# Separate waits for ScalarE's copy of B's rows and for VectorE's turns in a LoRA kernel

## The chip, the cores and the metric

The kernel runs on one core of a Trainium2 chip. The metric is device time in microseconds (us) of one execution; a lower time is better. A core has five engines that run programs of their own and meet only at semaphores: TensorE (PE in the profile, its weight loads PEld), VectorE (DVE), ScalarE (ACT), GpSimd (POOL) and SyncE (SP), which here issues all transfers between the chip's memory (HBM) and the on-chip buffer SBUF.

## What is computed

```
x: 16 x 512 x 768, A: 768 x 16, B: 16 x 768, scale = 0.5     (float32)
lora = np.matmul(np.matmul(x, A), B)
return (x + scale * lora).astype(np.float32)
```

x is 25.17 MB and is read once; the output is as large and is written once. The arithmetic between is small.

## The kernel before, in words

The 8192 rows (tokens) of x are cut into 64 tiles of 128 tokens; 8 tiles make a group, and there are NG = 8 groups. SBUF has room for 48 tiles, so x comes in by 8 loads (load 0 and load 1 hold group 0; loads 2, 3 and 4 a group each; load 5 two groups; loads 6 and 7 groups 6 and 7) and leaves by 5 stores (0 and 1 a group each, 2, 3 and 4 two groups each). The result is written in place over x, and loads 6 and 7 go into the room that stores 0 and 1 have emptied.

For each group g the work goes through five steps, each on an engine of its own:

1. The casts (`narrowed`, line 196): ScalarE casts tiles 0 to 3 of the group to fp16, GpSimd tiles 4 to 7. Each waits for its load and for `s_taken` >= g, which says that group g-1's fp16 copy `xn` has been turned and that PE has begun to read the turned tile `xt`. For ScalarE line 194 leaves this wait out at g = 1. Each cast raises `s_narrow`.
2. The turn (`turned`, line 256): VectorE transposes `xn` to `xt` in one instruction, and raises `s_turned`.
3. The projection (`projected`, line 286): 24 matmuls of `xt` with `w_bd`, a block-diagonal form of A, into the PSUM tile `ps_yt`. The second raises `s_taken`, the last `s_y`.
4. The muls (line 241): ScalarE writes the scaled projection to `y_bd` in four instructions. The first also raises `s_narrow` (not in the last group), the last `s_spread`.
5. The raising matmuls (`raised`, line 307) multiply `y_bd` with `b_mm` into two PSUM tiles `lora`, two token tiles at a time (a pair), and VectorE's four adds per group (line 261) add them to x in place. The last add of the groups at which a store ends raises `s_sum`.

VectorE's order is written out by hand (lines 271 to 276): the turn of group g+1 stands ahead of the four adds of group g. Its turn waits for `s_narrow` >= 3(g+1): two casts and the first mul of group g, which stands for the end of group g's projection, since `xt` may be overwritten only then. ScalarE's order is: cast of group g+1, muls of group g. PE's loop (lines 328 to 335) runs per group: pairs 0 and 1, the first half of the next projection, pairs 2 and 3, the second half.

B's rows come in at the start, GpSimd casts them (line 214), and PE spreads them over the partitions with two matmuls on `pick` (line 320) into `lora`'s first tile. ScalarE copies them out to `b_mm` (line 234). Before the change this copy waits for `s_taken` >= 1, which the second projection matmul of group 0 raises; PE runs in order, so the matmuls at line 320 are over by then. `b_mm` is waited for once, at line 327, ahead of PE's loop.

SyncE's program (lines 136 to 184) holds all transfers in one order: loads 0 to 5 at the start; stores 0 and 1 when `s_sum` has counted two and PE has raised pair 1 of group 2 (`s_lora` >= 10); load 6 when store 0 has landed, load 7 when store 1 has; store 2 when `s_sum` has counted three and `s_raise` six (PE has begun to raise group 5); store 3 when `s_sum` has counted four; the last store (line 356) after the last add.

Of the kernel before, what the change touches and what calls it, by code (L numbers as in the profile page):

```python
# [28 lines left out]
def kernel(  # L29
# [8 lines left out]
    nc = tc.nc  # L38
# [10 lines left out]
    NG = sum(PARTS) // GROUP  # L49
# [33 lines left out]
    def sem(name):  # L83
        sems.append(nc.alloc_semaphore(name))
        return sems[-1]
# [10 lines left out]
    def memory(t2, i, s, n):  # L96
        S = PARTS[i]
        return t2[ds(parts[i], S * P), :].rearrange("(p s) d -> p s d", s=S)[:, ds(s, n), :]

    def held(i, s, n):  # L100
        return tiles(where.index((i, s)), n)

    def tiles(t, n):
        return x_all[:, ds(t % ROOM, n), :]
# [6 lines left out]
    def load_of(t):  # L111
        i, s = where[t]
        return next(k for k, ld in enumerate(LOADS) if ld[0] == i and ld[1] <= s < ld[1] + ld[2])
# [1 line left out]
    assert SETS * SET == NC  # L115
    s_a, s_b = sem("s_a"), sem("s_b")
    s_ready, s_brows, s_pick = sem("s_ready"), sem("s_brows"), sem("s_pick")
    s_w, s_bh, s_bm = sem("s_w"), sem("s_bh"), sem("s_bm")
    s_first, s_narrow, s_turned, s_taken = sem("s_first"), sem("s_narrow"), sem("s_turned"), sem("s_taken")
    s_y, s_spread, s_lora = sem("s_y"), sem("s_spread"), sem("s_lora")  # L120

# [66 lines left out]
    def narrowed(e, copy, g, first, n=SUB):  # L188
        t = g * GROUP + first
        for k in dict.fromkeys(load_of(t + k) for k in range(n)):  # L190
            if (e, k) not in here:
                here.add((e, k))
                e.wait_ge(s_load[k], 16)
        if g > (e is nc.scalar):
            e.wait_ge(s_taken, g)
        ins = copy(out=xn[:, ds(first, n), :], in_=tiles(t, n))  # L196

        ins.then_inc(s_narrow if g else s_first if first else s_a, 1)

    def on_gpsimd(e):  # L200
        e.memset(a_rows[0:Q], 0.0).then_inc(s_ready, 1)  # L201
        e.memset(b_rows, 0.0).then_inc(s_brows, 1)  # L202
        e.memset(pick, 0.0).then_inc(s_pick, 1)
        e.memset(w_bd.rearrange("p c k m -> p (c k m)").bitcast(fp32), 0.0)  # L204
        e.memset(y_bd.rearrange("p s m -> p (s m)").bitcast(fp32), 0.0).then_inc(s_ready, 1)  # L205
        e.wait_ge(s_pick, 1)
        e.affine_select(  # L207
            out=pick, in_=pick, compare_op=mybir.AluOpType.not_equal, fill=1.0, base=0,
            pattern=[[0, NQ], [-APART, Q]], channel_multiplier=1,
        ).then_inc(s_pick, 1)  # L210
        narrowed(e, e.tensor_copy, 0, 0, SUB // 2)
        e.wait_ge(s_pick, 2)
        e.wait_ge(s_b, 16)
        e.tensor_copy(out=b_half, in_=b_rows).then_inc(s_bh, 1)  # L214
        e.wait_ge(s_ready, 3)
        e.tensor_copy(  # L216
            out=w_one.rearrange("i (c e) k r -> i c e (k r)", c=SETS),
            in_=a_t[0:Q].rearrange("i k r (e c) -> i c e (k r)", c=SET)[:, 0:SETS, 0:SET, :],
        ).then_inc(s_w, 1)
        e.wait_ge(s_w, 1)  # L220
        for b in range(NQ):
            e.tensor_copy(  # L222
                out=w_bd[ds(b * Q, Q), :, :, ds(b * Q, R)], in_=w_one
            ).then_inc(s_w, 1)
            e.wait_ge(s_w, b + 2)
        for g in range(1, NG):
            narrowed(e, e.tensor_copy, g, SUB)

    def on_scalar(e):
        narrowed(e, e.copy, 0, SUB // 2, SUB // 2)  # L230
        narrowed(e, e.copy, 0, SUB)

        e.wait_ge(s_taken, 1)
        e.copy(out=b_mm, in_=lora[0][:, 0, :]).then_inc(s_bm, 1)  # L234
        for g in range(NG):
            if g + 1 < NG:
                narrowed(e, e.copy, g + 1, 0)
            e.wait_ge(s_y, g + 1)
            for b in range(NQ):
                q = ds(b * Q, Q)  # L240
                last = e.mul(out=y_bd[q, :, q], in_=y_ps[q, :, :], mul=sc)  # L241
                if b == 0 and g + 1 < NG:

                    last.then_inc(s_narrow, 1)
            last.then_inc(s_spread, 1)

    def on_vector(e):
        e.wait_ge(s_a, SETS * 16 + 1)
        e.transpose(  # L249
            out=a_t[0:Q].rearrange("i k r c -> i (k r) c"),  # L250
            in_=a_rows[0:Q].rearrange("c (i k r) -> c (k r) i", k=2, r=R),
        ).then_inc(s_ready, 1)

        def turned(first, n):
            ts = [v[:, ds(first, n), :].bitcast(fp32) for v in (xt, xn)]
            return e.transpose(out=ts[0], in_=ts[1])  # L256

        def summed(g, p):
            xs = tiles(g * GROUP + 2 * p, 2)
            e.wait_ge(s_lora, g * PAIRS + p + 1)  # L260
            ins = e.tensor_tensor(out=xs, in0=xs, in1=lora[p % 2], op=mybir.AluOpType.add)  # L261
            if p + 1 == PAIRS and g in STORED:
                ins.then_inc(s_sum, 1)
            elif g + 1 < NG or p + 2 < PAIRS:
                ins.then_inc(s_free[p], 1)

        for h in range(2):
            e.wait_ge(s_first, h + 1)
            ins = turned(h * SUB, SUB)
        ins.then_inc(s_turned, 1)  # L270
        for g in range(NG):
            if g + 1 < NG:
                e.wait_ge(s_narrow, 3 * (g + 1))
                turned(0, GROUP).then_inc(s_turned, 1)
            for p in range(PAIRS):
                summed(g, p)

    def on_tensor(e):


        xv = xt.rearrange("p s (c j k) -> p s c j k", c=NC, k=2)

        def projected(first, last):
            for m in range(first, last):
                c, k = divmod(m, 2)
                mm = e.matmul(  # L286
                    y_ps, w_bd[:, c, k, :], xv[:, :, c, :, k],
                    start=(m == 0), stop=(m == MMS - 1),
                )
                if m == 0:  # L290
                    mm.then_inc(s_turned, -1)
                if m == 1:

                    mm.then_inc(s_taken, 1)
                if m == MMS - 1:
                    mm.then_inc(s_y, 1)

        def raised(p):
            if p == 0:
                e.wait_ge(s_spread, 1)  # L300
            free = s_free[(p + 2) % PAIRS]
            e.wait_ge(free, 1)
            t = lora[p % 2]
            mms = []
            for k in range(2):
                for n0, w in ((0, 512), (512, 256)) if k == 0 else ((0, 256), (256, 512)):
                    mms.append(e.matmul(  # L307
                        t[:, k, ds(n0, w)], y_bd[:, 2 * p + k, :], b_mm[:, ds(n0, w)],
                        start=True, stop=True,
                    ))  # L310
            if p == 0:
                mms[0].then_inc(s_raise, 1)
                mms[2].then_inc(s_spread, -1)
            mms[1].then_inc(free, -1)
            mms[-1].then_inc(s_lora, 1)

        e.wait_ge(s_pick, 2)
        e.wait_ge(s_bh, 1)
        for n0, w in ((0, 512), (512, 256)):
            last = e.matmul(  # L320
                lora[0][:, 0, ds(n0, w)], pick.rearrange("p b r -> p (b r)"),
                b_half[:, ds(n0, w)], start=True, stop=True,
            )
        e.wait_ge(s_w, 1 + NQ)
        e.wait_ge(s_turned, 1)
        projected(0, MMS)
        e.wait_ge(s_bm, 1)
        with e.Fori(0, NG - 1):
            raised(0)
            raised(1)  # L330
            e.wait_ge(s_turned, 1)
            projected(0, MMS // 2)
            raised(2)
            raised(3)
            projected(MMS // 2, MMS)
        for p in range(PAIRS):
            raised(p)

    on_sync(nc.sync)
    on_gpsimd(nc.gpsimd)  # L340
    on_scalar(nc.scalar)
    on_vector(nc.vector)
    on_tensor(nc.tensor)

    nums = [s.num for s in sems]
# [10 lines left out]
    last = nc.sync.dma_start(out=memory(out2, *STORES[-1]), in_=held(*STORES[-1]))  # L356
# [39 lines left out]
```

## Time and profile before

| | us |
|---|---|
| median of 3 runs (123.65 to 123.83) | 123.83 |
| the profiled execution | 123.56 |
| its span, first to last instruction | 121.6 |
| VectorE busy | 81.9 |
| PE busy | 51.1 |
| ScalarE busy | 37.4 |
| GpSimd busy | 28.4 |

The profile is one execution. Its times are given from the span's start; what lies around the span is 123.56 - 121.6 = 1.96 us. A row of the timeline has start, duration, engine, line, operation, tile written <- tiles read, and in brackets how long the engine was idle before and what ended it ("<-"). A row "x4" stands for four instructions in a row, its duration from the first's start to the last's end. In the view by stretches the columns are named in its first line, with the busy time of each engine in us; the DMA share is that of the 16 DMA engines, booked where a packet starts, so that it can pass 1. "DMA to landing" is the time from the start of an issue to the moment at which all its data is there. A small q behind an engine's name (ACTq) marks its sequencer, which runs standing waits (EVENT_SEMAPHORE) itself.

### The profile page before, as it was taken

The page shows a single profiled execution, that of the slowest core. Times are in us where ns is not written, and L with a number is a line of the kernel's source. Part 1 is how long each engine was busy: PE and PEld are TensorE (multiplying, and loading weights), DVE is VectorE, ACT ScalarE, POOL GpSimd, SP SyncE. Part 2 cuts the span into 40 slices and gives each one's busy share as a digit, 9 for nine tenths or more (in the row PEclk, how much of TensorE's full clock was granted, in tenths as well). Part 3 has the DMA queues.
Part 4 walks back from the last instruction along what each step waited for, and adds up shares of the span by engine and source line. Part 5 has one row for each costly group of instructions (what it writes and reads, how often), then busy time and mean ns, then how long its engine had stood idle before and what let it go on. Part 6 is the DMA issues. An engine that isn't in the chain of part 4 may idle for free.

```text
span 121.6 us, 888 instructions
## 1 busy us (share of the span) xinstructions
PE 51.1 (42%) x322; PEld 29.9 (25%) x322; DVE 81.9 (67%) x42; ACT 37.4 (31%) x43; POOL 28.4 (23%) x24
## 2 busy tenths in 40 slices
PE   0000239477457457747745725894574520000000
PEld 0000026244233324424423412552342110000000
DVE  0002950799999999999999969999996992000000
ACT  4003919535417402826240093634004000000000
POOL 7731638135017002606200080620000000000000
PEclk9999999999999999999999998599999998555555
DMA  3999999999998997999999999998999899899890
GB/s 59 436 430 449 445 420 428 445 420 420 477 517 356 420 517 315 428 428 445 420 420 445 436 412 485 420 517 372 404 517 404 372 517 404 372 517 420 356 517 0
DMA packets 1928, 50.43 MB, mean 415 GB/s; under 512 B 236, under 2 KB 236, under 8 KB 392
## 3 DMA queue, kind: packets, MB, share of 16 engines
q1 hardware_dynamic: 1928, 50.43, 97.0%
HBM read 25.26 MB, written 25.17 MB: 415 GB/s over the span
## 4 chain that ended last, share of the span: by engine, by line
DVE 32%; DMA 29%; PE 12%; ACT 9%; issue 1%; SPq 0%; POOLq 0%
DMA x_sb<-in_x_dram 20%; DVE x_sb L261 19%; DVE xt L256 12%; DMA out_dram<-x_sb 9%; PE ps_yt L286 8%; ACT xn L196 6%; PE lora_ps L307 4%; ACT y_bd L241 3%; SPq L139 0%; SPq L391 0%; POOLq L134 0%; POOLq L377 0%
## 5 line engine op out<-in xcount | busy, mean ns | idle before, releaser
L261 DVE TENSOR_TENSOR x_sb<-x_sb,lora_ps 128x1536 f32<-128x1536 f32 x32 | 53.8, 1736 | 1.5 <-PE lora_ps L307 1.4
L307 PE MATMUL lora_ps<-b_mm,y_bd 128*128 128x512 f16 (+1 forms) x128 | 25.1, 329 | 22.2 <-ACT y_bd L241 14.8
L196 ACT CAST xn<-x_sb 128x3072 f16<-128x3072 f32 (+1 forms) x9 | 23.4, 2609 | 34.5 <-DMA x_sb<-in_x_dram 21.7
L286 PE MATMUL ps_yt<-xt,w_bd 128*128 128x256 f16 x192 | 26.5, 291 | 12.9 <-DVE xt L256 12.9
L256 DVE STREAM_TRANSPOSE xt<-xn 128x3072 f32<-128x3072 f32 (+1 forms) x9 | 27.1, 3007 | 6.6 <-ACT y_bd L241 6.1
L196 POOL CAST xn<-x_sb 128x3072 f16<-128x3072 f32 (+1 forms) x8 | 20.7, 2586 | 45.1 <-DMA x_sb<-in_x_dram 23.4
L286 PEld LDWEIGHTS ps_yt<-xt,w_bd 128*128 128x128 f16 x192 | 19.1, 102 | 21.1 <-issue 16.2
L307 PEld LDWEIGHTS lora_ps<-b_mm,y_bd 128*128 128x128 f16 x128 | 10.6, 97 | 34.8 <-ACT y_bd L241 17.0
L241 ACT ACTIVATE y_bd<-ps_yt 32x256 f16<-32x256 f32 x32 | 12.0, 374 | 18.1 <-PE ps_yt L286 17.7
L249 DVE STREAM_TRANSPOSE a_t<-a_rows 32x1024 f32<-32x1024 f32 x1 | 2.0, 1975 | 11.3 <-DMA a_rows<-in_A_dram 11.3
L320 PE MATMUL lora_ps<-b_half,pick 128*128 128x512 f16 (+1 forms) x2 | 0.8, 501 | 12.5 <-POOL b_half L214 12.5
L320 PEld LDWEIGHTS lora_ps<-b_half,pick 128*128 128x128 f16 x2 | 0.1, 105 | 12.5 <-issue 12.5
L222 POOL COPY w_bd<-w_one 32x384 f16<-32x384 f16 x4 | 2.0, 500 | 0.2
L214 POOL CAST b_half<-b_rows 128x768 f16<-128x768 f32 x1 | 0.8, 827 | 4.4 <-DMA b_rows<-in_B_dram 4.4
L234 ACT CAST b_mm<-lora_ps 128x768 f16<-128x768 f32 x1 | 0.8, 799 | 2.6 <-PE ps_yt L286 2.6
L196 ACT ACT_TABLE_LOAD x1 | 1.3, 1283 | 0.9 <-PEq L377 0.9
L204 POOL MEMSET w_bd<- 128x1536 f32 x1 | 1.4, 1372 | 0.0
L201 POOL MEMSET a_rows<- 32x1024 f32 x1 | 0.9, 941 | 0.5 <-POOLq L134 0.5
L216 POOL CAST w_one<-a_t 32x384 f16<-32x384 f32 x1 | 0.9, 851 | 0.9 <-DVE a_t L249 0.9
L202 POOL MEMSET b_rows<- 128x768 f32 x1 | 0.7, 727 | 0.0
L205 POOL MEMSET y_bd<- 128x512 f32 x1 | 0.5, 514 | 0.0
L207 POOL TENSOR_SCALAR_AFFINE_SELECT pick<-pick 128x128 f16<-128x128 f16 x1 | 0.3, 298 | 0.0
(5 smaller groups left out, 0.6 us busy)
## 6 DMA issues: line engine op xcount, KB each, us to landing
out_dram<-x_sb SPq DMA_DIRECT2D x3, 6144.0 KB, 19.0
x_sb<-in_x_dram SPq DMA_DIRECT2D x5, 3072.0 KB, 14.6
x_sb<-in_x_dram SPq DMA_DIRECT2D x1, 6144.0 KB, 41.7
out_dram<-x_sb SPq DMA_DIRECT2D x2, 3072.0 KB, 14.4
x_sb<-in_x_dram SPq DMA_DIRECT2D x1, 2304.0 KB, 9.9
x_sb<-in_x_dram SPq DMA_DIRECT2D x1, 768.0 KB, 4.7
a_rows<-in_A_dram SPq DMA_DIRECT2D x3, 16.0 KB
b_rows<-in_B_dram SPq DMA_DIRECT2D x1, 48.0 KB, 7.5
```

The source lines that it names most:

```text
L196: ins = copy(out=xn[:, ds(first, n), :], in_=tiles(t, n))
L201: e.memset(a_rows[0:Q], 0.0).then_inc(s_ready, 1)
L204: e.memset(w_bd.rearrange("p c k m -> p (c k m)").bitcast(fp32), 0.0)
L216: e.tensor_copy(out=w_one.rearrange("i (c e) k r -> i c e (k r)", c=SETS), in_=a_t[0:Q].rearrange("i k r (e c) -> i c e (k r)", c=SET)[:, ...
L222: e.tensor_copy(out=w_bd[ds(b * Q, Q), :, :, ds(b * Q, R)], in_=w_one).then_inc(s_w, 1)
L241: last = e.mul(out=y_bd[q, :, q], in_=y_ps[q, :, :], mul=sc)
L249: e.transpose(out=a_t[0:Q].rearrange("i k r c -> i (k r) c"), in_=a_rows[0:Q].rearrange("c (i k r) -> c (k r) i", k=2, r=R),).then_inc(s_r ...
L256: return e.transpose(out=ts[0], in_=ts[1])
L261: ins = e.tensor_tensor(out=xs, in0=xs, in1=lora[p % 2], op=mybir.AluOpType.add)
L286: mm = e.matmul(y_ps, w_bd[:, c, k, :], xv[:, :, c, :, k], start=(m == 0), stop=(m == MMS - 1),)
L307: mms.append(e.matmul(t[:, k, ds(n0, w)], y_bd[:, 2 * p + k, :], b_mm[:, ds(n0, w)], start=True, stop=True,))
L320: last = e.matmul(lora[0][:, 0, ds(n0, w)], pick.rearrange("p b r -> p (b r)"), b_half[:, ds(n0, w)], start=True, stop=True,)
```

## The change

ScalarE's copy of B's rows gets a semaphore of its own, `s_bp`, raised by the last matmul at line 320. ScalarE's cast of group 1 now waits for `s_taken` >= 1 like GpSimd's (line 194), as the copy no longer does so ahead of it. The first mul no longer raises `s_narrow`; VectorE's turn waits for `s_y` >= g+1 and for `s_narrow` >= 2(g+1). An instruction carries one wait; a second wait becomes an instruction of its own ahead of it, so ScalarE's program has one instruction more and VectorE's seven. The order of all other instructions on every engine is the same.

```diff
-    s_w, s_bh, s_bm = sem("s_w"), sem("s_bh"), sem("s_bm")
+    s_w, s_bh, s_bp, s_bm = sem("s_w"), sem("s_bh"), sem("s_bp"), sem("s_bm")
...
-        if g > (e is nc.scalar):
+        if g:
             e.wait_ge(s_taken, g)
         ins = copy(out=xn[:, ds(first, n), :], in_=tiles(t, n))
...
         narrowed(e, e.copy, 0, SUB)
-
-        e.wait_ge(s_taken, 1)
+        e.wait_ge(s_bp, 1)
         e.copy(out=b_mm, in_=lora[0][:, 0, :]).then_inc(s_bm, 1)
...
                 last = e.mul(out=y_bd[q, :, q], in_=y_ps[q, :, :], mul=sc)
-                if b == 0 and g + 1 < NG:
-
-                    last.then_inc(s_narrow, 1)
             last.then_inc(s_spread, 1)
...
             if g + 1 < NG:
-                e.wait_ge(s_narrow, 3 * (g + 1))
+                e.wait_ge(s_y, g + 1)
+                e.wait_ge(s_narrow, 2 * (g + 1))
                 turned(0, GROUP).then_inc(s_turned, 1)
...
                 b_half[:, ds(n0, w)], start=True, stop=True,
             )
+        last.then_inc(s_bp, 1)
         e.wait_ge(s_w, 1 + NQ)
```

## The prediction

> **What bounds the kernel now.** I read the page first: the span, the DMA rows, the chain.
>
> ```profile
> span 121.6 us, 888 instructions
> ...
> DMA  3999999999998997999999999998999899899890
> ...
> q1 hardware_dynamic: 1928, 50.43, 97.0%
> ...
> DVE 32%; DMA 29%; PE 12%; ACT 9%; issue 1%; SPq 0%; POOLq 0%
> ```
>
> Two answers stand against each other here. The last line, the chain of waits, gives VectorE 32% and DMA 29%, as if the adds and turns set the end. The lines above it say that the DMA engines are busy in 97.0% of the span and move 50.43 MB, and that none of 40 slices but the first and the last is under 0.7. To choose between them I ask whether the transfers ever wait for the computation. The timeline of SyncE, which issues all transfers, gives the issue times; the views of single issuing lines give the time from an issue to its landing.
>
> ```profile
> 0.89 0.85 SPq L139 DMA_DIRECT2D x_sb<-in_x_dram  x2
> ...
> 44.15 0.82 SPq L149 DMA_DIRECT2D out_dram<-x_sb  x2
> 55.12 7.70 SPq L139 DMA_DIRECT2D x_sb<-in_x_dram  x2
> 74.55 9.02 SPq L149 DMA_DIRECT2D out_dram<-x_sb  x2
> 101.84 0.33 SPq L356 DMA_DIRECT2D out_dram<-x_sb  x1
> ```
>
> ```profile
> DMA to landing us min/median/max: 14.6/14.6/14.6
> ```
>
> ```profile
> DMA to landing us min/median/max: 17.0/17.0/17.0
> ```
>
> ```profile
> DMA to landing us min/median/max: 23.1/23.1/23.1
> ```
>
> ```profile
> DMA to landing us min/median/max: 19.0/19.0/19.0
> ```
>
> These are, in order, the views of load 7, store 2, store 3 and the last store (line 356), each alone. A row of two issues gives the second by its end: load 7 is issued 0.3 us before 55.12 + 7.70 = 62.82, at 62.5, and store 3 0.3 us before 74.55 + 9.02 = 83.57, at 83.2. When load 5 and load 6 landed is told by the casts that waited for them:
>
> ```profile
> 47.90 2.75 ACT L196 CAST xn<-x_sb 128x3072 f16<-128x3072 f32 x1 [5.30 <-DMA x_sb<-in_x_dram]
> ...
> 69.75 2.75 ACT L196 CAST xn<-x_sb 128x3072 f16<-128x3072 f32 x1 [7.32 <-DMA x_sb<-in_x_dram]
> 69.78 2.75 POOL L196 CAST xn<-x_sb 128x3072 f16<-128x3072 f32 x1 [11.11 <-DMA x_sb<-in_x_dram]
> ```
>
> Now every transfer can be laid against the one ahead of it. Stores 0 and 1 are issued at 44.15, and load 5 lands at 47.9. Load 6 is issued at 55.12, and store 1 lands where load 7's wait for it ends, at 62.5. Load 7 is issued there, and load 6 lands at 69.75. Store 2 is issued at 74.55, and load 7 lands at 62.5 + 14.6 = 77.1. Store 3 is issued at 83.2, and store 2 lands at 74.55 + 17.0 = 91.5. The last store is issued at 101.84, and store 3 lands at 83.2 + 23.1 = 106.3; the last store lands at 101.84 + 19.0 = 120.84, 0.8 us before the span's end. Each transfer is asked for 2.5 to 8.3 us before its predecessor is through, and the landings of 69.75, 77.1, 91.5, 106.3 and 120.84 are 7.35 us apart for 3072 KB and 14.4 to 14.8 for 6144 KB: one even stream. What remains is whether the computation slows that stream. The view by stretches of time answers it:
>
> ```profile
> core 0: us, PE busy (x) PEld busy (x) DVE busy (x) ACT busy (x) POOL busy (x), PEclk, DMA share, GB/s
> 1.00:2.00 1.00, 0.00 (x0) 0.00 (x0) 0.00 (x0) 1.00 (x1) 1.00 (x2) 1.00 0.42 49
> ...
> 24.00:36.00 12.00, 7.18 (x49) 4.19 (x48) 12.00 (x7) 4.25 (x5) 2.75 (x1) 1.00 1.04 449
> 106.00:118.00 12.00, 0.00 (x0) 0.00 (x0) 0.00 (x0) 0.00 (x0) 0.00 (x0) 0.50 1.02 442
> ```
>
> With VectorE busy throughout, 449 GB/s; with no engine busy at all, 442. The stream doesn't feel the engines. So the kernel is bound by 50.43 MB through one full queue, and the chain's VectorE share is work that ends while the queue still has something to do.
>
> **The change, part by part.** First, ScalarE's copy of B's rows (line 234) no longer waits for group 0's second projection matmul but for the two matmuls at line 320; in exchange a wait for that projection stands ahead of ScalarE's cast of group 1. Second, VectorE's turn of group g+1 is released by the end of group g's projection (and the two casts), not by the first of ScalarE's four muls on it; that is one standing wait more ahead of each of seven turns. Nothing else is added on any engine: no DMA, no arithmetic, and the new signal of the matmul is an increment on an instruction that is there already. The rows around group 1:
>
> ```profile
> 12.55 0.80 PE L320 MATMUL lora_ps<-b_half,pick 128*128 128x512 f16 x2 [12.55 <-POOL b_half L214]
> ...
> 17.95 0.80 ACT L234 CAST b_mm<-lora_ps 128x768 f16<-128x768 f32 x1 [2.58 <-PE ps_yt L286]
> 18.76 2.75 ACT L196 CAST xn<-x_sb 128x3072 f16<-128x3072 f32 x1
> 18.85 2.74 POOL L196 CAST xn<-x_sb 128x3072 f16<-128x3072 f32 x1 [2.44 <-DMA x_sb<-in_x_dram]
> 21.79 1.54 ACT L241 ACTIVATE y_bd<-ps_yt 32x256 f16<-32x256 f32 x4 [0.28 <-PE ps_yt L286]
> 22.19 3.38 DVE L256 STREAM_TRANSPOSE xt<-xn 128x3072 f32<-128x3072 f32 x1 [5.01 <-ACT y_bd L241]
> ```
>
> *The copy.* Its matmuls end at 13.35. ScalarE was idle for 2.58 us before the copy, that is from 17.95 - 2.58 = 15.37; there the copy will stand, 2.6 us earlier, and end at 16.2. The copy's result is first read by the raising matmuls (line 307), which also wait for ScalarE's muls from 21.79 on, so an earlier copy brings PE nothing. Queued behind the new wait on ScalarE are the cast of group 1 and the four muls. The wait ends at 17.95, when the copy was released until now. The cast then waits for load 2, as GpSimd's cast beside it did until 18.85; it had begun at 18.76, right behind the copy. So it begins at 18.76 or a little before; best case 17.95 (0.81 us), worst case later by one wait instruction. I take 0, since load 2 is what GpSimd's row names. Even the best case is worth nothing, because the turn also needs GpSimd's cast (18.85 + 2.74 = 21.59) and the projection, which ends just ahead of the muls at 21.79.
>
> *The turns.* The price of a standing wait comes from rows of the same kind:
>
> ```profile
> L195 POOLq EVENT_SEMAPHORE  x6: 17/17/816, 17.9 to 77.1; - x6
> L195 ACTq EVENT_SEMAPHORE  x5: 17/17/17, 26.1 to 77.1; - x5
> ```
>
> A wait that is already met costs 17 ns in its own row; the longest, 816 ns, is GpSimd's at 17.9, which really waited, for load 2. For VectorE's the ends are therefore 0 and 0.82 us each; I take at most 0.1, the row of waits that were met being the nearest. Turn 1: begins at 21.79 plus up to 0.1 in place of 22.19, a gain of 0.30 to 0.40. Turns 2 to 5 and 7: VectorE is not idle before them. Two neighbours show it:
>
> ```profile
> 31.13 1.54 ACT L241 ACTIVATE y_bd<-ps_yt 32x256 f16<-32x256 f32 x4 [2.17 <-PE ps_yt L286]
> 32.13 3.36 DVE L256 STREAM_TRANSPOSE xt<-xn 128x3072 f32<-128x3072 f32 x1
> ```
>
> The projection has ended by 31.13 and the turn begins at 32.13, straight behind VectorE's adds: an earlier release gains 0 there, and the new wait is met 1.0 us before VectorE is free, so its 17 ns lie beside the adds too. Behind each new wait on VectorE stand its turn and four adds, and behind them PE's projection and the stores; the 1.0 us is the cover. Turn 6 is the other place with idle time:
>
> ```profile
> 72.53 1.54 ACT L241 ACTIVATE y_bd<-ps_yt 32x256 f16<-32x256 f32 x4
> 72.93 3.38 DVE L256 STREAM_TRANSPOSE xt<-xn 128x3072 f32<-128x3072 f32 x1 [1.06 <-ACT y_bd L241]
> ```
>
> The two casts of group 6 end at 69.75 + 2.75 = 72.50 and 69.78 + 2.75 = 72.53; the turn can begin there, 0.30 to 0.40 earlier. These two gains don't add up at the end: turn 6 hangs on load 6, which lands after store 0, at a time that the stream sets. So the adds behind turn 6, and the last store's issue, come about 0.35 us earlier: 101.5.
>
> *The sum.* VectorE's work ends 0.35 us sooner. Stores 0 and 1 are asked for some 0.35 us sooner than 44.15, with load 5 still moving until 47.9; store 2's issue follows ScalarE's muls behind load 6 and doesn't move; the last store is asked for 4.8 us, not 4.5, before store 3 has landed. None of it moves a byte earlier. Gain on the span: 0; loss: 0. Against the profiled execution's own 123.56 us (span 121.6) the sum is 123.56. The median of the runs shown is 123.83, 0.27 higher; carried to it, the forecast is 123.8 us.
>
> **The rivals.** *VectorE's chain is the bound after all (faster).* For it: the chain of waits gives VectorE 32%, more than DMA. Then the time falls by what turn 1 and turn 6 gain: at most 0.40 + 0.40 = 0.8 us, 123.0, and by the smaller value 0.6, 123.2. Against it: the last store waits 4.5 us in the queue, and the landings are evenly spaced. The Trainium skill, "Perfetto Trace Analysis", section "Identifying the Most-Contended Engine", speaks for this rival: it says that occupancy is misleading for DMA because there are 16 engines, so that 97.0% by itself would prove nothing; by that rule read alone the chain's first name, VectorE, would be the one to shorten. The even landings above are a row of another kind, and they hold without the 97.0%.
>
> *The standing waits hold VectorE up (slower).* Place: the seven turns; price c each. The last store's issue slips by 7c, less the 0.40 gained at turn 1, less the 1.06 us of idle before turn 6: 7c - 1.46. A transfer's bytes move at most 1.1 us after its issue (issue at 0.89, DMA already 0.42 busy in the stretch from 1 to 2), so the queue is covered up to 106.3 - 101.84 - 1.1 = 3.4 us, and the rival decides from c = 0.69 us. At the upper end, 0.82, the slip is 4.28, 0.9 us over the cover: 123.8 + 0.9 = 124.7. Against it: 17 ns in every wait of this kind that was met. The Trainium skill, "Perfetto Trace Analysis", section "Sequencer-only Instruction (DRAIN, etc)", speaks for it: such an instruction's wait is served in the sequencer, which reads the next instruction only after it, so what stands behind cannot even be queued. The rows of ScalarE's waits show only their 17 ns, and no row of VectorE here shows such a wait in the loop.
>
> *The change doesn't move the turns.* If a met wait cost VectorE 0.4 us at turn 1 and turn 6, the muls' release would be replaced by one as late: c = 0.4 makes 7c - 1.46 = 1.3 us of slip, inside the 3.4 of cover, and the time is again 123.8.
>
> **How the numbers follow.** Earlier turns behind a full queue: 0.80. Turns unmoved or late inside the cover: 0.08; same time. VectorE's chain as the bound: 0.05. Waits that break the cover: 0.05. I keep 0.01 on each side for a start of the stream that differs. About 0.2% (0.25 us) is what a measurement of this kernel can tell from no change, so: faster 0.06, same 0.88, slower 0.06. The runs shown lie from 123.65 to 123.83 and the profiled one at 123.56; the forecast's own scatter, with 0.25 us above the median for the same on that side, gives 123.5 to 124.1. That leaves out 123.0 to 123.2 and 124.7, about 0.12 together.
>
> **What would show it.** Copy of B's rows near 15.4; cast of group 1 still at about 18.7; turn 1 at 21.8 to 21.9; turn 6 within 0.1 us of GpSimd's cast's end; all other turns straight behind the adds; the last store issued near 101.5 and landing near 120.8, its time in the queue longer by what the issue gained; 97% on the DMA queue. It would be wrong if the last landing moved with VectorE's end (the first rival), if idle time stood before VectorE's turns 2 to 5 (the second), or if the landings' spacing of 7.35 and 14.5 us changed, for which I have no mechanism.

## The result and the profile after

The changed kernel takes 123.48 us (median of 22 runs, 123.21 to 123.77), the kernel before 123.67 us (22 runs, 123.49 to 124.11); the ratio is 0.9986, with a 95% interval of 0.9979 to 0.9992. That is a gain of 0.14%, which the interval keeps clear of zero, and the time lies 0.02 us below the stated range. The forecast of no change was wrong, by little.

The page of the changed kernel, in the rows that the prediction began with:

```profile
span 121.7 us, 896 instructions
...
DMA  3999999999997996999999999997998998998890
...
q1 hardware_dynamic: 1928, 50.43, 97.1%
...
DMA 29%; DVE 28%; PE 15%; ACT 9%; issue 2%; SPq 0%; POOLq 0%
```

The first row is a surprise. The span is 121.7 us, no shorter than the 121.6 of before, and yet this very execution took 123.44 us against 123.56. Unrounded, the two traces have spans of 121.654 and 121.622 us, so what became shorter is what lies around the span: 123.44 - 121.654 = 1.79 us against 1.94 (1.96 by the rounded span). Eight instructions are more in the program (896 against 888), as the change says. The DMA queue is as full as before.

SyncE's timeline and, from the views of store 2, store 3 and the last store alone, the times to landing:

```profile
44.27 0.82 SPq L149 DMA_DIRECT2D out_dram<-x_sb  x2
55.19 7.82 SPq L139 DMA_DIRECT2D x_sb<-in_x_dram  x2
74.79 9.51 SPq L149 DMA_DIRECT2D out_dram<-x_sb  x2
102.58 0.33 SPq L354 DMA_DIRECT2D out_dram<-x_sb  x1
```

```profile
DMA to landing us min/median/max: 16.8/16.8/16.8
```

```profile
DMA to landing us min/median/max: 22.4/22.4/22.4
```

```profile
DMA to landing us min/median/max: 18.3/18.3/18.3
```

The last store is issued at 102.58, 0.74 us later than before, and lands at 102.58 + 18.3 = 120.88; before, it landed at 120.84. It waited less in the queue by what it came later. Store 2 lands at 74.79 + 16.8 = 91.6 and store 3, issued 0.3 us before 74.79 + 9.51 = 84.30, at 106.4, where they landed before (91.5 and 106.3).

The timeline around group 1's turn shows the two edits at work:

```profile
15.31 0.80 ACT L233 CAST b_mm<-lora_ps 128x768 f16<-128x768 f32 x1
...
17.24 5.04 PE L283 MATMUL ps_yt<-xt,w_bd 128*128 128x256 f16 x24 [3.76 <-DVE xt L252]
18.82 2.75 ACT L196 CAST xn<-x_sb 128x3072 f16<-128x3072 f32 x1 [2.71 <-DMA x_sb<-in_x_dram]
18.91 2.74 POOL L196 CAST xn<-x_sb 128x3072 f16<-128x3072 f32 x1 [2.36 <-DMA x_sb<-in_x_dram]
22.32 1.54 ACT L240 ACTIVATE y_bd<-ps_yt 32x256 f16<-32x256 f32 x4 [0.75 <-PE ps_yt L283]
22.32 3.38 DVE L252 STREAM_TRANSPOSE xt<-xn 128x3072 f32<-128x3072 f32 x1 [5.23 <-PE ps_yt L283]
```

The copy of B's rows stands at 15.31 instead of 17.95. The turn begins with the first mul, at 22.32, no longer 0.4 us behind it, and its releaser is the projection. The projection, though, took 5.04 us in this execution against 4.42 in the one before, so the turn begins 0.13 us later than 22.19. Such a difference needs no change of the kernel: in a second profiled execution of the kernel before (e1 below) the projection took 5.25 us and the turn began at 22.85.

```profile
17.16 5.25 PE L286 MATMUL ps_yt<-xt,w_bd 128*128 128x256 f16 x24 [3.90 <-DVE xt L256]
...
22.85 3.38 DVE L256 STREAM_TRANSPOSE xt<-xn 128x3072 f32<-128x3072 f32 x1 [5.83 <-ACT y_bd L241]
```

Turn 6 and what follows it on VectorE:

```profile
69.81 2.75 POOL L196 CAST xn<-x_sb 128x3072 f16<-128x3072 f32 x1 [11.02 <-DMA x_sb<-in_x_dram]
72.56 1.54 ACT L240 ACTIVATE y_bd<-ps_yt 32x256 f16<-32x256 f32 x4
72.67 3.38 DVE L252 STREAM_TRANSPOSE xt<-xn 128x3072 f32<-128x3072 f32 x1 [0.67 <-POOL xn L196]
...
75.97 3.38 DVE L257 TENSOR_TENSOR x_sb<-x_sb,lora_ps 128x1536 f32<-128x1536 f32 x2
80.44 3.42 DVE L257 TENSOR_TENSOR x_sb<-x_sb,lora_ps 128x1536 f32<-128x1536 f32 x2 [1.09 <-PE lora_ps L304]
```

It begins 0.11 us behind the first mul's start and 0.26 us earlier than before. Then VectorE loses it all again: 1.09 us of waiting for PE, whose granted clock was lower from 74 to 78.5 us here (0.50 against 0.65). The rows of two stretches in the view by stretches, first the changed kernel's, then those of before (columns as in the prediction):

```profile
17.00:22.40 5.40, 5.04 (x24) 3.27 (x24) 0.17 (x2) 2.83 (x2) 2.74 (x1) 1.00 1.01 432
74.00:78.50 4.50, 4.35 (x17) 2.46 (x18) 4.50 (x3) 1.19 (x2) 1.05 (x1) 0.50 1.22 524
```

```profile
17.00:22.40 5.40, 4.42 (x24) 2.96 (x24) 0.39 (x2) 4.14 (x4) 2.74 (x1) 1.00 1.00 428
74.00:78.50 4.50, 3.68 (x18) 2.18 (x19) 4.50 (x3) 1.44 (x2) 1.32 (x1) 0.65 1.21 519
```

In the stretch from 74 us the column PEclk is 0.50 against 0.65; in the first stretch it is 1.00 in both, though the same 24 matmuls took 5.04 and 4.42 us. So in these two executions the change's VectorE chain ended later, not earlier, and the kernel was faster all the same.

### The profile page after: what moved, and what is told of

Read it like the earlier page. It is cut to its first block, busy times and chain, and to the rows that moved or that the text cites. A ratio compares the mean times of both kernels' runs of the same rounds, so it can differ in the third digit from the quotient of the medians.

```text
span 121.7 us, 896 instructions
## 1 busy us (share of the span) xinstructions
PE 52.9 (43%) x322; PEld 30.9 (25%) x322; DVE 81.8 (67%) x42; ACT 37.5 (31%) x43; POOL 28.4 (23%) x24
## 4 chain that ended last, share of the span: by engine, by line
DMA 29%; DVE 28%; PE 15%; ACT 9%; issue 2%; SPq 0%; POOLq 0%
DMA x_sb<-in_x_dram 20%; DVE x_sb L257 18%; DVE xt L252 10%; DMA out_dram<-x_sb 9%; PE ps_yt L283 8%; PE lora_ps L304 6%; ACT xn L196 6%; ACT y_bd L240 4%; SPq L139 0%; SPq L389 0%; POOLq L134 0%; POOLq L375 0%
## 5 line engine op out<-in xcount | busy, mean ns | idle before, releaser
L304 PE MATMUL lora_ps<-b_mm,y_bd 128*128 128x512 f16 (+1 forms) x128 | 26.4, 343 | 22.1 <-ACT y_bd L240 14.7
L283 PE MATMUL ps_yt<-xt,w_bd 128*128 128x256 f16 x192 | 27.3, 296 | 11.8 <-DVE xt L252 11.8
L283 PEld LDWEIGHTS ps_yt<-xt,w_bd 128*128 128x128 f16 x192 | 19.5, 104 | 20.2 <-issue 14.9
L304 PEld LDWEIGHTS lora_ps<-b_mm,y_bd 128*128 128x128 f16 x128 | 11.2, 102 | 35.3 <-ACT y_bd L240 16.9
L240 ACT ACTIVATE y_bd<-ps_yt 32x256 f16<-32x256 f32 x32 | 12.0, 375 | 19.1 <-PE ps_yt L283 18.7
## 6 DMA issues: line engine op xcount, KB each, us to landing
out_dram<-x_sb SPq DMA_DIRECT2D x3, 6144.0 KB, 18.3
```

The source lines that it names most:

```text
L283: mm = e.matmul(y_ps, w_bd[:, c, k, :], xv[:, :, c, :, k], start=(m == 0), stop=(m == MMS - 1),)
L304: mms.append(e.matmul(t[:, k, ds(n0, w)], y_bd[:, 2 * p + k, :], b_mm[:, ds(n0, w)], start=True, stop=True,))
```

## The experiments

Theory A: the 0.19 us between the medians lies outside the span, and comes with the length of a program, not with any earlier release. Theory B: the turns are released earlier and the span is shorter. The measure that tells them apart is each run's time less its span, averaged over the runs of a kernel. Spans are listed to 0.1 us, which by itself scatters a single difference by 0.05 either way; nearly all of the scatter of 0.03 (one standard deviation) of most kernels is that, and a mean over 8 to 33 runs is then good to about 0.01. In e5, e6, e7, e8, e10 and e18 the runs scatter by 0.06 to 0.13, and their means are good to 0.02 to 0.04. The spans of the 22 runs of before beside the changed kernel are not on record; the first row stands for them, with runs of the same kernel beside the experiments.

```
kernel                      ScalarE     runs   mean    time less span
                            instr. more        span    mean  (lowest-highest)
before, beside all of these 0           133    121.71  1.94  (1.89-1.99)
changed kernel              1            22    121.71  1.78  (1.73-1.83)
e1  before again            0            11    121.69  1.94  (1.89-1.99)
e2  copy alone              1, early     11    121.73  1.77  (1.73-1.81)
e3  turns alone             0            11    121.67  1.94  (1.89-1.97)
e4  padded, no release      1, early     11    121.64  1.79  (1.74-1.82)
e14 one wait                1, early      9    121.80  1.78  (1.73-1.83)
e15 two waits               2, early      8    121.76  1.87  (1.81-1.90)
e18 three waits             3, early      8    121.70  1.97  (1.80-2.15)
e5  one wait                1, late      10    121.77  1.82  (1.73-1.93)
e6  two waits               2, late      10    121.63  2.24  (1.87-2.36)
e7  three waits             3, late       8    121.70  2.04  (1.93-2.12)
e8  four waits              4, late       8    121.69  1.95  (1.88-2.05)
e13 five waits              5, late       9    121.74  1.90  (1.85-1.93)
e16 eight waits             8, late       8    121.69  1.90  (1.85-1.94)
e10 changed + 3 late        4            10    121.71  2.00  (1.89-2.10)
e11 one wait on GpSimd      0             8    121.79  1.93  (1.88-1.96)
e12 one wait on SyncE       0             8    121.79  1.95  (1.91-1.98)
e17 one wait on PE          0             8    121.73  1.95  (1.89-1.98)
```

The experiments ran in five lots, each on a chip of its own, with runs of the kernel before beside them; in each lot those gave 1.93 or 1.94 outside the span on the mean. "Early" is ahead of the casts of group 1 or of the copy of B's rows, "late" ahead of ScalarE's last four muls.

### The parts, and the length without the parts (e1 to e4)

e1 is the kernel before as it stands.

> The kernel before, unchanged, for the time outside its span over many executions. Theory A (the 0.19 us between the medians, 123.67 and 123.48, lies outside the span and comes with the programs' length): ratio 1.000, spans near 121.7 like those of the changed kernel, so that time less span is about 1.96 us, as in the profile of before, against 1.78 in the changed kernel's runs. Theory B (the turns are released earlier and the span is shorter): time less span about 1.78, like the changed kernel, and spans near 121.9.

Measured: 123.65 us, ratio 0.9995 (0.9981 to 1.0009); 1.94 us outside the span. As theory A has it.

e2 is the copy's part alone (against the kernel before, as all edits below but e10's):

```diff
+        last.then_inc(s_bp, 1)               # the matmuls at line 320
...
-        if g > (e is nc.scalar):
+        if g:
             e.wait_ge(s_taken, g)
...
-        e.wait_ge(s_taken, 1)
+        e.wait_ge(s_bp, 1)
         e.copy(out=b_mm, in_=lora[0][:, 0, :]).then_inc(s_bm, 1)
```

> The copy of B's rows alone: its own semaphore, and the standing wait ahead of ScalarE's cast of group 1; the turns wait as before. One instruction more on ScalarE, none on VectorE. Theory A: between 0 and -0.19 us, all of it outside the span; 0 if VectorE's length is what counts. Theory B: 1.000, since the turns are not moved.

Measured: 123.46 us, ratio 0.9989 (0.9979 to 0.9999), span unchanged on the mean (121.73), 1.77 us outside. The one instruction more on ScalarE brings the whole 0.16 us.

e3 is the turns' part alone:

```diff
-                if b == 0 and g + 1 < NG:
-
-                    last.then_inc(s_narrow, 1)
...
-                e.wait_ge(s_narrow, 3 * (g + 1))
+                e.wait_ge(s_y, g + 1)
+                e.wait_ge(s_narrow, 2 * (g + 1))
```

> The turns alone: release by the projection's end, seven standing waits more on VectorE; the copy as before. Theory A: if VectorE's length counts, -0.19 us (ratio 0.9985) with an unchanged span. Theory B: -0.19 us too, but in the span.

Measured: 123.6 us, ratio 0.9994 (0.9982 to 1.0007), 1.94 us outside, mean span 121.67. Seven instructions more on VectorE do nothing around the span, so theory A falls in the form in which VectorE's length counts. The interval of the ratio by itself would still allow theory B's 0.9985. What speaks against B is that the changed kernel, which has the same releases, has the span of before (121.71 us in both), and e10 below.

e4 has the change's number of instructions on both engines and none of its releases:

```diff
-        if g > (e is nc.scalar):
+        if g:
             e.wait_ge(s_taken, g)
...
+                e.wait_ge(s_y, g + 1)
                 e.wait_ge(s_narrow, 3 * (g + 1))
```

> The programs' length of the changed kernel without its earlier releases: the copy and the first mul wait and signal as before, and one standing wait on ScalarE and seven on VectorE stand where the change has them. Theory A: -0.19 us (ratio 0.9985), outside the span. Theory B: 1.000 or slower, since nothing is released earlier.

Measured: 123.39 us, ratio 0.9979 (0.9970 to 0.9988), 1.79 us outside: the gain of the change without anything that the change is for. (The ratio is lower still than the change's, by a mean span that is 0.13 us under that of the runs beside it; I take that for chance, as the time outside is that of the change.) Its profile bears on the cover, too. Page, timeline, and the view of the last store alone:

```profile
span 121.9 us, 896 instructions
```

```profile
17.20 5.28 PE L287 MATMUL ps_yt<-xt,w_bd 128*128 128x256 f16 x24 [3.99 <-DVE xt L256]
...
23.00 3.38 DVE L256 STREAM_TRANSPOSE xt<-xn 128x3072 f32<-128x3072 f32 x1 [5.95 <-ACT y_bd L241]
...
44.96 0.82 SPq L149 DMA_DIRECT2D out_dram<-x_sb  x2
...
101.62 0.33 SPq L357 DMA_DIRECT2D out_dram<-x_sb  x1
```

```profile
DMA to landing us min/median/max: 19.5/19.5/19.5
```

Turn 1 begins at 23.00, 0.81 us later than before, behind a projection of 5.28 us, and stores 0 and 1 are issued as much later, at 44.96; load 6 is asked for all the same in time, at 54.98. The last store lands at 101.62 + 19.5 = 121.1, 0.3 us later than before. That this isn't the late turn's doing is seen by two other executions. e2's has its turn 1 as late and the shortest span of all profiles; e10's (below) has the earliest turn, released by GpSimd's cast, and a longer span.

```profile
span 121.5 us, 889 instructions
...
23.00 3.38 DVE L255 STREAM_TRANSPOSE xt<-xn 128x3072 f32<-128x3072 f32 x1 [5.87 <-ACT y_bd L240]
```

```profile
span 121.8 us, 899 instructions
...
21.57 3.38 DVE L254 STREAM_TRANSPOSE xt<-xn 128x3072 f32<-128x3072 f32 x1 [4.55 <-POOL xn L196]
```

### ScalarE's number of instructions (e5 to e8, e13, e16)

Each adds n instructions that only wait for something long met. Such an instruction takes up to two waits, so 2n - 1 waits make n of them, the muls' own wait being the last; the pages count 889, 890, 891 and 892 instructions for e5 to e8 against 888. In e5 to e8 all waits are on `s_taken`, which is the same code for up to eight of them:

```diff
+            for k in range(2 * n - 1 if g + 1 == NG else 0):
+                e.wait_ge((s_taken, s_lora)[k // 8], k % 8 + 1)
             e.wait_ge(s_y, g + 1)
```

> The kernel before with one standing wait more on ScalarE, long met, ahead of its last four muls; all else unchanged. Theory A, in the form that the runs so far leave (ScalarE's count of instructions sets a time outside the span, wherever the instruction stands): time less span 1.78 us instead of 1.94, ratio 0.9987, span unchanged. Rival A2 (it is the wait's place ahead of the cast of group 1 that counts): time less span 1.94, ratio 1.000.

Measured: 1.82 us outside (seven of ten runs from 1.73 to 1.82, three at 1.91 to 1.93), 123.55 us, ratio 0.9997 (0.9986 to 1.0008), span 121.77. The number outside the span follows theory A, though not in every run; the ratio alone would not have told.

> The same place, two standing waits more on ScalarE. If the count counts as a step (any program longer than before), time less span is 1.78 us; if it goes by every second instruction, it is back at 1.94; if each instruction takes off the same, 1.62.

Measured: 2.24 us outside, 123.93 us, ratio 1.0020 (1.0008 to 1.0031). None of the three forms that I had written down: slower than before, by 0.30 us outside an unchanged span. Its page and result side by side: the profiled execution took 123.97 us.

```profile
span 121.7 us, 890 instructions
```

The same span as the changed kernel's profile (123.44 us), and 0.53 us more.

> Three standing waits more on ScalarE at the same place. As a step: 1.78 us outside the span; every second instruction: 1.78; the same from each: 1.46.

Measured: 2.04 us outside, 123.8 us, ratio 1.0007 (0.9994 to 1.0020). Again none of them.

> Four standing waits more on ScalarE at the same place. As a step: 1.78 us outside the span; every second instruction: 1.94; every fourth: 1.94; the same from each: 1.30.

Measured: 1.95 us outside, 123.67 us, ratio 1.0002 (0.9990 to 1.0013). After four the value of before is back on the mean, which suggested a rule modulo four; the next two runs were for that. A first form of five, e9, has no time: it took all nine waits from `s_taken`, which counts to eight, so the ninth was never met. e13 takes the ninth from `s_lora`.

> The kernel before with five standing waits more on ScalarE ahead of its last four muls. So far the time less the span is 1.94 us as it was, 1.78 to 1.82 with one instruction more on ScalarE, 2.24 with two, 2.04 with three, 1.95 to 2.00 with four. If it goes by the count modulo four, five give 1.78 to 1.82 again. If four is only where it levels off: 1.94 to 2.0.

Measured: 1.90 us outside, 123.61 us, ratio 1.0000 (0.9990 to 1.0011). The rule modulo four falls.

> Eight standing waits more on ScalarE at the same place. By the count modulo four: time less span 1.94 to 2.0 us. If each step is its own: any value from 1.75 to 2.3, which would leave the rule open.

Measured: 1.90 us outside, 123.56 us, ratio 0.9993 (0.9982 to 1.0004). That lies outside the 1.94 to 2.0 of the rule as well; with e13 against it, no rule is left.

### The place of the instruction (e14, e15, e18)

n instructions more ahead of the copy of B's rows, which itself waits as before:

```diff
+        for k in range(2 * n - 1):
+            e.wait_ge(s_load[1], 15 - k)
         e.wait_ge(s_taken, 1)
```

> The kernel before with one standing wait more on ScalarE, long met, ahead of its copy of B's rows instead of ahead of its last muls; the copy itself waits as before. If the number alone counts: time less span 1.78 to 1.82 us, as with the changed kernel and with the late place. If the place counts: 1.94.

Measured: 1.78 us outside, 123.53 us, ratio 0.9990 (0.9973 to 1.0007). The fourth kernel with one early instruction more, and the fourth at 1.77 to 1.79.

> Two standing waits more on ScalarE ahead of its copy of B's rows. If the number alone counts: time less span 2.24 us as with the late place, ratio about 1.002, slower than before. If the place counts: another value.

Measured: 1.87 us outside, 123.54 us, ratio 0.9997 (0.9980 to 1.0015); the late place gave 2.24. So the place counts beside the number.

> Three standing waits more on ScalarE ahead of its copy of B's rows. One gave 1.78 us outside the span there, two 1.87. If the early place rises with the number: about 1.95. If it goes as the late place (2.04 with three): about 2.04.

Measured: 1.97 us outside, with single runs from 1.80 to 2.15, 123.65 us, ratio 0.9999 (0.9986 to 1.0013). Nearer to the first of the two values, but at this scatter it settles nothing.

### The change kept, its length altered (e10)

The changed kernel with three late instructions more on ScalarE (the edit of e5 with five waits):

> The changed kernel, earlier releases and all, with three standing waits more ahead of ScalarE's last four muls: four instructions more on ScalarE than before. Theory A (count of ScalarE's instructions alone): time less span back at 1.95 us, ratio 1.000 although every release of the change is kept. Theory B: ratio 0.9986, as the change has it.

Measured: 2.00 us outside, 123.69 us, ratio 1.0007 (0.9998 to 1.0017). Every release of the change is kept, and its gain is gone. Together with e4 this is the cross: length without releases has the gain, releases with another length haven't.

### The other engines (e11, e12, e17)

One instruction more that waits for something long met: on GpSimd ahead of its last cast, on SyncE ahead of its wait for store 1, on PE ahead of its loop.

```diff
+            for k in range(2 if g + 1 == NG else 0):        # e11, GpSimd
+                e.wait_ge(s_w, k + 1)
             narrowed(e, e.tensor_copy, g, SUB)
...
+        for k in range(1):                                  # e12, SyncE
+            e.wait_ge(s_lora, k + 1)
         e.wait_ge(s_out1, 16)
...
+        for k in range(1):                                  # e17, PE
+            e.wait_ge(s_w, k + 1)
         e.wait_ge(s_bm, 1)
```

> The kernel before with one standing wait more on GpSimd, long met, ahead of its last cast. If only ScalarE's program counts: time less span 1.94 us. If any program's length does: another value than 1.94, by 0.1 us or more.

Measured: 1.93 us outside, 123.75 us, ratio 1.0009 (0.9997 to 1.0021).

> The kernel before with one standing wait more on SyncE, long met, ahead of its wait for store 1. If only ScalarE's program counts: time less span 1.94 us. If any program's length does: another value, by 0.1 us or more.

Measured: 1.95 us outside, 123.72 us, ratio 1.0011 (1.0001 to 1.0021). The interval just misses 1, but by a mean span of 121.79 against 121.66 of the runs beside it, not by the time around the span.

> The kernel before with one standing wait more on PE, long met, ahead of its loop. If only ScalarE's program counts: time less span 1.94 us. If PE's counts as well: another value, by 0.1 us or more.

Measured: 1.95 us outside, 123.7 us, ratio 1.0002 (0.9990 to 1.0013). With e3 that makes four engines whose programs were lengthened, each in one way, without a mark outside the span. Of the lengths and places tried, ScalarE's alone count; another place or number on those four was not tried.

No version beats the changed kernel beyond its interval: e4 (123.39), e2 (123.46) and e14 (123.53) have the same time outside the span by one instruction more on ScalarE.

## Why the prediction was wrong

*The bound* was right. The transfers are one full stream: the changed kernel's last store was issued 0.74 us later than before and landed at 120.9 all the same; e2's and e4's turns began 0.81 us late, and e10's 0.62 early, and their spans follow neither (121.5, 121.9 and 121.8). The mean spans of the 17 experiments lie from 121.63 to 121.80 us without following any release.

*The copy.* Forecast at 15.4 with group 1's cast still at 18.7: found at 15.31 and 18.82, the cast now waiting for load 2 by name. Right.

*The turns.* The mechanism was right: turn 1 begins at the projection's end, turn 6 0.11 us after GpSimd's cast (72.56), and the standing waits leave no idle time ahead of the others. VectorE's own row of the new waits, and two of those turns in its timeline:

```profile
L270 DVEq EVENT_SEMAPHORE  x7: 21/21/21, 21.7 to 81.1; - x7
```

```profile
32.26 3.36 DVE L252 STREAM_TRANSPOSE xt<-xn 128x3072 f32<-128x3072 f32 x1
...
83.77 3.37 DVE L252 STREAM_TRANSPOSE xt<-xn 128x3072 f32<-128x3072 f32 x1
```

Neither turn has a bracket, so VectorE was not idle before it; the other three of turns 2 to 5 and 7 have none either. The times 21.8 to 21.9 and the last store's 101.5 were wrong, since I carried PE's times over from one execution: group 0's projection took 5.04 us instead of 4.42, and the clock granted at 74 to 78.5 was 0.50 instead of 0.65. Neither reached the end. So the forecast of the last landing, 120.8, held although the store was issued 1.1 us later than forecast, and not 0.3 earlier than before: the time in the queue became shorter, not longer.

*The step that failed* is the sum: "Against the profiled execution's own 123.56 us (span 121.6) the sum is 123.56." It took the 1.96 us around the span (unrounded 1.94) as given. They are a term of the time like any other, and the one term that this change altered: 1.78 against 1.94 us, a fall of 0.16, of the 0.19 between the medians; the other 0.03 is within what mean spans differ by (121.71 us for the changed kernel and for all runs of before, 121.63 to 121.80 among the experiments). The sentence "Nothing else is added on any engine" counted instructions by what they cost where they stand, 17 ns beside other work; e4 and e14 show that one of them counted by being there. I had weighed what the seven waits on VectorE could hold up, and had counted the single one on ScalarE at its place alone, where it holds nothing up.

*A second error of the same size:* the base. 123.83 was a median of three; over 22 runs it is 123.67. Of the 0.35 us between 123.83 and the 123.48 measured, 0.16 is the base and 0.19 the change. With the better base, the same working and the same 0.33 us of room below, the range would have reached 123.34. It would have held the result by luck, with the term around the span still taken as fixed.

*The rivals.* VectorE's chain as the bound (123.0 to 123.2) did not come: e3 has all of its releases and stays at 0.9994. The rule of the Trainium skill that I had put beside it, "Perfetto Trace Analysis", section "Identifying the Most-Contended Engine", I had read by half: it goes on to judge DMA by HBM utilization in place of occupancy, so it does not by itself name VectorE. Here the queue that was 97% occupied was the bound. Waits that hold VectorE up (124.7) did not come either. By the Trainium skill, "Perfetto Trace Analysis", section "Sequencer-only Instruction (DRAIN, etc)", such a wait is served in the sequencer, which takes up the next instruction only after it. VectorE's seven held nothing up all the same: 21 ns each in the row above, and no idle time before the turns behind the adds. ScalarE's rows stay at 17 ns, now six of them:

```profile
L195 ACTq EVENT_SEMAPHORE  x6: 17/17/17, 17.9 to 77.4; - x6
```

That the change might not move the turns was refuted by their releasers. None of the rivals was the cause that decided.

*Where the time lies.* The traces also hold semaphore updates and DMA packets from outside the span, and these place the difference behind it, in the one profiled execution of each kernel. Every execution closes with nine updates of one semaphore, number 2. In the six kernels that leave ScalarE's length alone (before, e1, e3, e11, e12, e17) the last of the nine comes 2.02 us behind the span's end; in the five with one instruction more (changed, e2, e4, e5, e14) it comes at 1.90 to 1.91. The first seven of the nine come at the same times in all eleven; the eighth follows the seventh by 0.15 us in the six and by 0.03 in the five. By unrounded spans the time less span is 1.93 to 1.94 us in the six and 1.78 to 1.79 in the five.

Longer programs show something else. In the seven kernels with two late or three and more instructions, and in no other, a packet of 8192 bytes that the trace calls "instruction" moves behind the span. Its end and the time less span, both in us of the same execution:

```
kernel   packet ends behind the span   time less span
e6                2.52                     2.29
e7                2.34                     2.10
e8                2.28                     2.04
e18               2.17                     1.93
e10               2.11                     1.90
e13               1.61                     1.90
e16               1.13                     1.90
```

In the first four the time ends 0.24 us before the packet does, whatever its end; in the last three it is 1.90. So the long times of e6, e7 and e8 go with a late fetch of instructions. That the kernel waits for this packet is read from these times; no run leaves the packet out.

*What stays open.* Why one instruction more, with no such packet, brings the last two updates 0.11 to 0.12 us forward, and where the other 0.04 of the 0.16 lies; why two early ones give 1.87, with no packet either; and why e5 has two values. That the time outside the span depends on the number and place of ScalarE's added waits is shown. All instructions that were added are standing waits; whether another kind would do the same was not tried.

## What to carry to other kernels

Split the time into span and rest before explaining a difference of a few tenths of a microsecond, and compare the rest over many runs: here it held nearly all of the difference, and the span none. A small gain from a change of waits should be tried against the same number of instructions without the change; e4 was that kernel, and showed that the gain belongs to the one instruction added and not to what it waits for. Where transfers form one full stream, each asked for some microseconds before its turn (here 2.5 to 8.3), releasing the computation a few tenths of a microsecond earlier buys nothing.

## What the runs showed of the hardware that was not expected

- The time outside the span is no constant: 1.77 to 2.24 us on the mean, by the number and place of standing waits in ScalarE's program, and unmoved (1.93 to 1.95) by one instruction more on GpSimd, SyncE or PE and by seven more on VectorE, in the places tried.
- With a few instructions more in ScalarE's program, 8192 bytes marked "instruction" are moved behind the span: seven of the 19 traces have that packet, ending 1.13 to 2.52 us behind the span's end, and where it ended at 2.17 or later the time ended 0.24 us before it.
- It can have two values within one kernel: e5 gave 1.73 to 1.82 in seven runs and 1.91 to 1.93 in three, e6 2.23 to 2.36 in nine and 1.87 in one.
- PE's first projection, the same 24 matmuls, took 4.42 and 5.25 us in two profiled executions of the kernel before (the second is e1's), 5.04 in that of the changed kernel and 5.28 in e4's, with a granted clock of 1.00 in the stretch from 17 to 22.4 us in all four.
